# Multiplying rows by their reciprocal root mean square on GpSimd in place of VectorE

## The chip, the core and the metric

The kernel runs on one core of a Trainium2 chip, as one launch. The metric is the device time of that launch in microseconds (us). Engines are named as in the profile: PE is TensorE's matmul, PEld its weight load, DVE is VectorE, ACT is ScalarE, POOL is GpSimd, SP is the engine that issues the DMAs.

## What is computed

A batch of one with 256 tokens of width 1024, in float32, goes through two layers of a first block (four kinds of attention, then a mixture of 16 experts) and two layers of a second block. The second block is where the change lies. It has two layers of three sublayers each: a gated feed-forward network, a mixer (an mLSTM in the first layer, a Mamba-2 scan in the second) and another feed-forward network. Cut to what matters:

```
def rms_norm(x, g):
    y = x * rsqrt(mean(x * x, axis=-1) + EPS)
    return y * g

def sublayer(x, fn, g_pre, g_post, shift, scale, gate, weight):
    hmod = rms_norm(x, g_pre) * (1 + scale) + shift
    y = rms_norm(fn(hmod), g_post)
    return x + weight * gate * y
```

In the Mamba-2 mixer the scan's output, multiplied by silu(z), is normed in the same way within each of four groups of 512 columns before the last projection.

## The kernel before

The 256 tokens are two row tiles, t = 0 and t = 1, of 128 partitions each. A matmul needs the activations with the contracted dimension on the partitions, so the function `make_xT` brings rows into that form. It takes four blocks of 128 columns at a time (a group, 512 columns), transposes them on PE into one PSUM bank (line 204), and takes them from there into SBUF as two parts: a rounded part `xTh`, cast by ACT (line 397), and the rest `xTl`, a subtraction on DVE (line 398). Three matmuls, of the two parts with the two parts `hi` and `lo` of the weights, then make one product (line 200). The weights' parts are made in the same way: ACT casts `hi` (line 290) and DVE subtracts to get `lo` (line 293); both inputs of that subtraction lie in SBUF.

Where `make_xT` is given a factor `r`, one per row, it first multiplies the group by it into a tile named `rr` (line 381); PE then transposes `rr`. Two places give it a factor:

- `sub_pre`, at the entry of each of the six sublayers, for each t: two groups of 512 columns, so 24 multiplies. ACT sums the squares (line 1470), DVE adds the two sums (line 245), POOL raises the result to the power -1/2 (line 246), and that is `r`. After the transposes, DVE (first group, line 393) and ACT (second group, line 395) put scale and shift on, into `xTm`.
- `gate` in `mamba`, for four groups of 512 columns and each t: one multiply each, so eight. There DVE makes the mean (line 236) and POOL the power (line 238).

A sublayer's last matmuls run over t = 0 first, then t = 1, and `sub_pre` for t is called as soon as the rows of t are done. So the entry of t = 0 runs beside the matmuls of t = 1, and the entry of t = 1 beside the next sublayer's first matmuls on t = 0. The first of the six entries follows a layer norm (lines 918 to 932; its factor comes from POOL's line 238) that ends the first block.

The order of the instructions on each engine is put together by a planner, from the order of the program, priorities that the code sets in places, and its own estimates of what each instruction takes. Each engine then runs its own list in that order and waits on semaphores. All loads of weights are issued from SP's queue; POOL issues no DMA here.

Of the kernel before, what the change touches and what calls it, by code (L numbers as in the profile page):

```python
# [16 lines left out]
OP = mybir.AluOpType  # L17
# [3 lines left out]
P = 128  # L21
# [113 lines left out]
class K:  # L135
# [236 lines left out]
    def make_xT(self, rows, t, xT, kt=KT, r=None, k0=0, mod=None, bank=None, hold=None):  # L372

        nc = self.nc
        for g in range(0, kt, 4):
            m = min(4, kt - g)
            ps = (bank or self.ps_tr)()[:, :m * P].rearrange("p (j q) -> p j q", j=m)
            c = rows[:, g * P:(g + m) * P]
            if r is not None:
                c = self.take([m * P], "rr")  # L380
                nc.vector.tensor_scalar(c, rows[:, g * P:(g + m) * P], r, None, OP.mult)
            for j in range(m):
                self.tr(ps[:, j], c[:, j * P:(j + 1) * P])
            if r is not None:
                self.give(c)
            i, o = divmod(k0 + g, 4)
            h, l = (x[i][:, o:o + m, t * P:(t + 1) * P] for x in xT)
            if mod is not None:
                src = self.take([4, P], "xTm")
                for j in range(m):  # L390
                    a, b = mod[1][:, g + j:g + j + 1], mod[0][:, g + j:g + j + 1]
                    if g == 0:
                        nc.vector.tensor_scalar(src[:, j], ps[:, j], a, b, OP.mult, OP.add)  # L393
                    else:
                        nc.scalar.activation(src[:, j], ps[:, j], AF.Identity, bias=b, scale=a)  # L395
                ps = src[:, :m]
            first = nc.scalar.copy(h, ps)  # L397
            second = nc.vector.tensor_sub(l, ps, h.bitcast(F32))  # L398
            if mod is not None:
                self.entry = second  # L400
            if hold:
                self.holds = {"s": [[EARLY_S, None], [99, first]], "v": [[MID_V, second]]}
            if mod is not None:
                self.give(src)
# [1614 lines left out]
```

## Time and profile before

| | us |
|---|---|
| median of three runs | 2161.49 |
| lowest and highest of the three | 2154.83, 2166.03 |
| the profiled execution's own time | 2156.63 |
| its span, first to last instruction | 2154.9 |

| engine | busy us | share of the span | instructions |
|---|---|---|---|
| PE | 2009.5 | 93% | 10417 |
| PEld | 1463.1 | 68% | 10417 |
| DVE | 1226.0 | 57% | 2049 |
| ACT | 834.2 | 39% | 1359 |
| POOL | 63.4 | 3% | 108 |

The span is one execution's; 1.7 us of the execution's own time lie outside it. Busy shares are averages over stages that differ, and work on one engine overlaps that on the others, so the columns don't add up to the span. What one instruction is worth is read from the wait that ends last at its place.

### The profile page before, as it was taken

Reading aid. Unit: us, or ns where it says so; the run is one execution under the profiler, and the core shown is the slowest. Engines: PE = TensorE matmul, PEld = TensorE weight load, DVE = VectorE, ACT = ScalarE, POOL = GpSimd, SP = SyncE. Lnnn points to the kernel's source line nnn. Section 1 sums busy time; section 2 is a strip of 40 time slices with the busy share of each in tenths; the row PEclk is TensorE's granted clock in tenths of the full one; section 3 lists DMA queues with packets and bytes.
Section 4 is the critical chain, followed back from the end, with each engine's and each line's share of the span. In section 5 each row is a group of like instructions: output and inputs, shape, how many; then the busy total and the mean of one; then the engine's idle time right before and its main releaser. Section 6 shows DMA issues by size and latency. Waiting matters only on the chain.

```text
span 2154.9 us, 28260 instructions
## 1 busy us (share of the span) xinstructions
PE 2009.5 (93%) x10417; PEld 1463.1 (68%) x10417; DVE 1226.0 (57%) x2049; ACT 834.2 (39%) x1359; POOL 63.4 (3%) x108
## 2 busy tenths in 40 slices
PE   7998899989997999979998979999999898998998
PEld 6866543338776443257786867777778797876887
DVE  5876411137776311177657776677667578655544
ACT  5543100024443100054334554345444456745442
POOL 1000000010000000000000000000000000000000
PEclk9998899999998999989998989999999999999999
DMA  6854799986755999968847746874786343334662
GB/s 226 318 160 150 278 410 411 411 335 226 256 176 193 364 409 410 410 207 272 270 161 262 254 147 203 275 261 150 252 281 219 110 129 117 104 136 143 188 209 82
DMA packets 214232, 515.85 MB, mean 239 GB/s; under 512 B 23562, under 2 KB 36936, under 8 KB 214088
## 3 DMA queue, kind: packets, MB, share of 16 engines
q1 hardware_dynamic: 214088, 513.98, 68.4%
q8 instruction: 84, 1.38, 0.3%
q14 instruction: 60, 0.49, 0.1%
HBM read 512.87 MB, written 1.05 MB: 238 GB/s over the span
## 4 chain that ended last, share of the span: by engine, by line
PE 45%; DMA 4%; DVE 4%; ACT 2%; issue 1%; POOL 0%; SPq 0%; DVEq 0%; POOLq 0%; ACTq 0%
PE ps L200 39%; PE ps L122 4%; DMA w<-in_ffn_w_dram 2%; DVE lo L293 2%; PE ps L204 1%; DMA w<-in_mb_w_in_dram 1%; DMA adaw<-in_ada_w_dram 1%; ACT hi L290 1%; DMA w<-in_ml_w_in_dram 1%; DVE xTm L393 0%; DVE lo L297 0%; ACT xTm L395 0%; DVE xTl L398 0%; PE ps L1411 0%; DVE adac L1447 0%
## 5 line engine op out<-in xcount | busy, mean ns | idle before, releaser
L200 PE MATMUL ps<-hi,xTh 128*128 128x512 f32 (+3 forms) x1632 | 641.7, 397 | 38.4 <-ACT xTh L397 24.0
L200 PE MATMUL ps<-hi,xTl 128*128 128x512 f32 (+3 forms) x1632 | 636.3, 390 | 7.5 <-DVE xTl L398 7.2
L293 DVE TENSOR_TENSOR lo<-w,hi 128x1024 fp32r<-128x1024 f32 (+2 forms) x458 | 482.0, 1074 | 271.1 <-ACT hi L290 261.5
L290 ACT CAST hi<-w 128x1024 fp32r<-128x1024 f32 (+2 forms) x458 | 416.3, 931 | 511.4 <-DMA w<-in_ffn_w_dram 331.4
L200 PE MATMUL ps<-lo,xTh 128*128 128x512 f32 (+3 forms) x1632 | 611.1, 387 | 0.9 <-DVE lo L293 0.6
L200 PEld LDWEIGHTS ps<-hi,xTh 128*128 128x128 f32 x1632 | 315.6, 194 | 112.6 <-ACT xTh L397 29.8
L200 PEld LDWEIGHTS ps<-hi,xTl 128*128 128x128 f32 x1632 | 316.8, 194 | 76.9 <-DVE xTl L398 13.6
L200 PEld LDWEIGHTS ps<-lo,xTh 128*128 128x128 f32 x1632 | 313.2, 192 | 66.2 <-DVE lo L293 2.0
L200 PE MATMUL ps<-w,xe 128*32 128x512 f32 (+2 forms) x1088 | 222.8, 597 | 1.7 <-DMA w<-in_w_dram 1.5
L1447 DVE SCALAR_TENSOR_TENSOR adac<-adaw,cact,adac 128x512 f32<-128x512 f32 x252 | 187.4, 748 | 13.8 <-DMA adaw<-in_ada_w_dram 9.8
L200 PEld LDWEIGHTS ps<-w,xe 128*32 128x32 f32 (+2 forms) x1088 | 65.5, 124 | 131.0 <-issue 110.4
L200 PE MATMUL ps<-w,hT 128*32 128x512 f32 (+2 forms) x520 | 132.8, 599 | 0.0
L122 PE MATMUL ps<-xTh,hi 128*128 128x256 f32 x384 | 112.4, 294 | 7.3 <-DVE dr L559 3.5
L122 PE MATMUL ps<-xTh,lo 128*128 128x256 f32 x384 | 111.3, 290 | 0.4 <-DVE lo L293 0.4
L122 PE MATMUL ps<-xTl,hi 128*128 128x256 f32 x384 | 109.9, 288 | 0.0
L1206 DVE TENSOR_TENSOR h<-h,ps 128x512 f32<-128x512 f32 (+1 forms) x14 | 9.6, 687 | 144.9 <-PE ps L200 143.7
L1228 ACT ACTIVATE yh<-ps,gs 128x512 fp32r<-128x512 f32 (+1 forms) x28 | 18.9, 686 | 186.0 <-PE ps L200 185.5
L200 PEld LDWEIGHTS ps<-w,hT 128*32 128x32 f32 (+2 forms) x520 | 38.0, 123 | 72.4 <-issue 59.4
L122 PEld LDWEIGHTS ps<-xTh,hi 128*128 128x128 f32 x384 | 75.2, 197 | 8.9 <-issue 4.0
L397 ACT CAST xTh<-ps 128x512 fp32r<-128x512 f32 (+1 forms) x84 | 42.7, 523 | 92.8 <-PE ps L204 89.7
L1229 DVE SCALAR_TENSOR_TENSOR yl<-ps,gs,yh 128x512 fp32r<-128x512 f32 (+1 forms) x28 | 20.7, 749 | 101.5 <-ACT yh L1228 101.0
L122 PEld LDWEIGHTS ps<-xTh,lo 128*128 128x128 f32 x384 | 75.4, 196 | 0.8 <-DVE lo L293 0.5
(350 smaller groups left out, 2014.2 us busy)
## 6 DMA issues: line engine op xcount, KB each, us to landing
w<-in_w_dram SPq DMA_DIRECT2D x378, 512.0 KB, 10.1
w<-in_ffn_w_dram SPq DMA_DIRECT2D x264, 512.0 KB, 4.6
adaw<-in_ada_w_dram SPq DMA_DIRECT2D x144, 512.0 KB, 4.9
w<-in_w_in_dram SPq DMA_DIRECT2D x60, 512.0 KB, 6.2
w<-in_mb_w_in_dram SPq DMA_DIRECT2D x40, 512.0 KB, 4.2
w<-in_ml_w_in_dram SPq DMA_DIRECT2D x24, 512.0 KB, 5.7
w<-in_w_out_dram SPq DMA_DIRECT2D x16, 512.0 KB, 5.7
w<-in_mb_w_out_dram SPq DMA_DIRECT2D x16, 512.0 KB, 3.3
```

What stands on the lines that cost most here:

```text
L122: self.k.nc.tensor.matmul(out, lhsT, rhs, start=not self.started, stop=stop)
L200: self.nc.tensor.matmul(out, lhsT, rhs, start=start, stop=stop)
L204: self.nc.tensor.transpose(out, in_, self.ident[:n, :n])
L290: self.nc.scalar.copy(hi[:, k], w[:, k])
L293: self.nc.vector.tensor_sub(lo[:, k], w[:, k], hi[:, k].bitcast(F32))
L397: first = nc.scalar.copy(h, ps)
L1206: V.tensor_mul(h[:m], h[:m], hp[1][:m])
L1228: nc.scalar.mul(yh[:m], py[n][:m], g)
L1229: V.scalar_tensor_tensor(yl[:m], py[n][:m], g, yh[:m].bitcast(F32), OP.mult, OP.subtract)
L1447: nc.vector.scalar_tensor_tensor(prev, wt[:, k], cc, prev, OP.mult, OP.add)
```

## The change

The multiply by `r` at line 381 goes to GpSimd. Operands, shapes and result stay as they are; the power on GpSimd (lines 238 and 246) stays where it is, so the factor is now made and used on the same engine.

```diff
             c = rows[:, g * P:(g + m) * P]
             if r is not None:
                 c = self.take([m * P], "rr")
-                nc.vector.tensor_scalar(c, rows[:, g * P:(g + m) * P], r, None, OP.mult)
+                nc.gpsimd.tensor_scalar(c, rows[:, g * P:(g + m) * P], r, None, OP.mult)
             for j in range(m):
                 self.tr(ps[:, j], c[:, j * P:(j + 1) * P])
```

## Rows read from the trace of the kernel before

**Rows 1.** Busy time by stretch; the second begins ahead of the first multiply.

```profile
core 0: us, PE busy (x) PEld busy (x) DVE busy (x) ACT busy (x) POOL busy (x), PEclk, DMA share, GB/s
925.00:2154.90 1229.90, 1153.79 (x5848) 947.37 (x5846) 812.88 (x1207) 584.42 (x900) 23.70 (x40) 0.96 0.59 191
```

**Rows 2.** The page's chain that ended last, shares by engine.

```profile
PE 45%; DMA 4%; DVE 4%; ACT 2%; issue 1%; POOL 0%; SPq 0%; DVEq 0%; POOLq 0%; ACTq 0%
```

**Rows 3.** DVE by line and shape: count, busy us and mean ns, idle before.

```profile
L293 DVE TENSOR_TENSOR lo<-w,hi 128x512 fp32r<-128x512 f32 x120 | 76.8, 685 | 29.1 <-ACT hi L290 29.1
...
L381 DVE TENSOR_SCALAR rr<-x,sm 128x512 f32<-128x512 f32 x24 | 10.6, 482 | 4.8 <-POOL sm L246 4.8
...
L381 DVE TENSOR_SCALAR rr<-y,sm 128x512 f32<-128x512 f32 x8 | 3.8, 480 | 1.5 <-POOL sm L238 1.5
```

**Rows 4.** Everything on tile rr: who waited for it (us, times).

```profile
  PE ps L204: 16.4, 4
...
  PEld ps L204: 2.6, 1
```

**Rows 5.** POOL by line and shape, its memsets.

```profile
L548 POOL MEMSET fqT<- 64x512 f32 x4 | 2.1, 520 | 17.2 <-PE ps L200 17.0
...
L1604 POOL MEMSET ur<- 128x128 f32 x2 | 0.4, 206 | 11.9 <-DVE xTl L398 11.3 <-ACT sq L1470 0.6
```

**Rows 6.** POOL's power on one column: ns of one, least/median/most.

```profile
L246 POOL TENSOR_TENSOR sm<-sm,cf x24: 550/551/1466, 933.7 to 2149.6; 128x1 f32<-128x1 f32 x24
```

**Rows 7.** The same for the power on four columns.

```profile
L620 POOL TENSOR_TENSOR sm<-sm,cf x16: 1007/1008/1502, 90.0 to 685.6; 128x4 f32<-128x4 f32 x16
```

**Rows 8.** Timeline at 1294 us: start us, us, engine, line, count [idle before].

```profile
1294.70 1.28 DVE L293 TENSOR_TENSOR lo<-w,hi 128x512 fp32r<-128x512 f32 x2
...
1294.93 1.47 POOL L246 TENSOR_TENSOR sm<-sm,cf 128x1 f32<-128x1 f32 x1 [4.99 <-DVE sm L245]
```

**Rows 9.** Timeline of POOL at the first entry.

```profile
933.72 0.55 POOL L246 TENSOR_TENSOR sm<-sm,cf 128x1 f32<-128x1 f32 x1 [3.11 <-DVE sm L245]
934.24 0.64 POOL L238 TENSOR_TENSOR sm<-sm,cf 128x1 f32<-128x1 f32 x1
938.73 0.55 POOL L246 TENSOR_TENSOR sm<-sm,cf 128x1 f32<-128x1 f32 x1 [3.86 <-DVE sm L245]
```

**Rows 10.** The chain from 929 to 957 us: start us, us, what.

```profile
935.04 0.88 DVE rr L381 x2
935.92 1.32 DVE x L932 x2
...
939.72 0.48 DVE rr L381
...
950.42 3.38 DVE lo L293 x6
...
954.72 0.61 DVE xTl L398
```

**Rows 11.** The chain from 1154 to 1167 us.

```profile
1155.69 1.42 DVE adac L1447 x2
1157.11 0.79 DVE rr L381 x2
...
1163.21 0.61 DVE xTl L398
```

**Rows 12.** The chain from 1698 to 1711 us.

```profile
1703.70 0.56 POOL sm L246
...
1704.29 0.50 DVE rr L381
...
1704.92 1.96 PE ps L204 x8
```

**Rows 13.** Timeline of PE: transposes of rr, with PE's idle time ahead of them.

```profile
939.86 1.11 PE L204 MATMUL ps<-cf,rr 128*128 128x128 f32 x4 [2.25 <-DVE rr L381]
...
1157.65 1.06 PE L204 MATMUL ps<-cf,rr 128*128 128x128 f32 x8 [0.25 <-DVE rr L381]
...
1505.48 1.03 PE L204 MATMUL ps<-cf,rr 128*128 128x128 f32 x8
...
1704.92 1.94 PE L204 MATMUL ps<-cf,rr 128*128 128x128 f32 x8 [4.08 <-DVE rr L381]
```

**Rows 14.** Timeline of DVE at 1504 us.

```profile
1504.06 0.88 DVE L381 TENSOR_SCALAR rr<-x,sm 128x512 f32<-128x512 f32 x2 [0.73 <-POOL sm L246]
```

## Prediction, made before the changed kernel was run

> **What bounds the kernel now.** I read the page's chain of waits first. PE carries most of what it names, DMA and DVE 4% each, POOL nothing [rows 2]. So the kernel is bound by TensorE's own work, and an elementwise instruction counts only where PE stands still for it. Next I read busy time by stretch. Nothing that the change touches runs ahead of 925 us; behind it PE is busy for 1153.8 of 1229.9 us [rows 1], so all of PE's idle time there is 1229.9 - 1153.8 = 76.1 us, and DVE, the engine that is relieved, is busy for 812.9, or 66%. Then I asked for everything on the tile rr: PE waited for it four times, 16.4 us together, and its weight load once [rows 4]. The reader is to see there that 20 chains hang on that tile (twelve entries, eight gates of the Mamba mixer), and PE stands still for it at four of them. Last I took the chain around these four to see whether the multiply, or what stands ahead of it, makes the wait [rows 10 to 12].
>
> **What leaves DVE.** 24 multiplies of 10.6 us and eight of 3.8 us [rows 3]: 14.4 us of DVE time. In pairs they overlap, two in 0.88 us [rows 14]. DVE's own idle time in front of them, waiting for POOL's power, is 4.8 + 1.5 = 6.3 us more [rows 3].
>
> **What POOL takes on.** The trace of before has no multiply on POOL, so its cost is bounded by POOL's nearest rows. From below: a memset of 512 columns takes 0.52 us, one of 128 columns 0.206 [rows 5], so 0.314 / 384 = 0.82 ns a column. An instruction that also reads won't be shorter than that, and 0.52 us is the lower end. For the fixed part of one that reads: the power takes 0.55 us on one column and 1.01 on four [rows 6, 7], so 0.153 us a column and 0.55 - 0.15 = 0.40 us besides. The column price of the power can't be that of one multiply: it would make 0.40 + 512 x 0.153 = 78.7 us of each, where DVE's multiply, one pass, costs 0.48 [rows 3]; that end I exclude, since a power is worked out in many steps and a product in one. I take fixed part plus one pass, 0.40 + 512 x 0.00082 = 0.82 us, as the multiply is nearest to the memset: a stream over 512 columns. The upper end is reading and writing one after the other, 0.40 + 2 x 0.42 = 1.24 us. So POOL gains 32 x 0.82 = 26 us on 23.7 busy ones in this stretch [rows 1] and is still nearly empty. It issues no DMA, so no load stands behind the multiplies; what does stand there is the next power.
>
> **Where a slower multiply is hidden.** POOL can start when its own power ends, with no trip to DVE's queue. Sixteen of the 20 chains have room: PE comes to the transposes later, in its own order, with no idle time in front of them. The tightest is at 1504 us. There DVE starts at 1504.06 [rows 14] and PE transposes at 1505.48 without idle time [rows 13]. POOL would have the first group at 1504.06 + 0.82 = 1504.88, the second at 1505.70, and PE needs the second half-way through its 1.03 us, at about 1505.9. So 0.2 us are left there, and at 1.24 us a multiply (second group at 1506.54) some 0.6 would be lost. The other fifteen have at least 1.4 us.
>
> **The four places that count.**
>
> (a) and (b), the first entry, 933 to 957 us. The chain is on DVE nearly throughout: two multiplies in 0.88 us, the layer norm of t = 1 behind them, the last multiply of t = 1 (0.48), then the subtractions and xTl, and PE waits for that [rows 10]. DVE is freed of 2 x 0.88 = 1.76 us there. Against it: t = 0's power ends at 934.27, and the power for t = 1's layer norm stands next on POOL and ends at 934.88 [rows 9]. If the two multiplies get in front of it, it ends at about 934.3 + 2 x 0.82 + 0.55 = 936.5, and the layer norm (935.92 now) starts some 0.6 us later. And t = 1's own multiply comes 0.82 - 0.48 = 0.34 us later to PE, which stands idle for it already [rows 13]. The subtractions of the weights, which need neither, can fill part of that. I put it at 1.76 - 0.6 - 0.34 = 0.8 us won; with all filled 1.76 are won, and with 1.24 us a multiply, 0.84 us later on top, none.
>
> (c) the second entry's t = 1, 1155 to 1164 us. Here the multiplies stand behind DVE's accumulations for another stage (1.42 us) and cost 0.79 us of DVE's chain, which ends in xTl and releases PE [rows 11]. Off DVE, 0.79 is the most that can be won; POOL has the power at 1156.2 and could be done at 1156.2 + 0.82 = 1157.0, ahead of DVE's 1157.5. I take 0.6 us, since ACT's part of the entry also stands in front of PE; at the lower end nothing.
>
> (d) the fifth entry's t = 1, 1704 us. The power ends at 1704.26, DVE's first product is there 0.5 us later, and PE, idle for 4.08 us, starts at once [rows 12, 13]. Nothing else is on DVE. POOL's product takes 0.82: 0.34 us lost, 0.76 at the upper end, next to nothing at the lower.
>
> The sum: - 0.8 - 0.6 + 0.34 = - 1.1 us. With POOL at 0.52 it is - 1.76 - 0.79 = - 2.6; with POOL at 1.24, 0 + 0 + 0.76 + 0.6 (the place at 1504) = + 1.4. Against the profiled execution's own time that is 2156.6 - 1.1 = 2155.5. That execution lies 4.9 us below the median of the runs shown, 2161.5, so as a median I expect 2160.4, and write 2160.
>
> **Contention, a rule that speaks against the change.** Rows first: a power on POOL that takes 0.55 us took 1.47 where two subtractions with both inputs in SBUF ran on DVE; it ended 0.42 us behind the second [rows 6, 8]. So POOL is held while such an instruction runs on DVE. Whether DVE is held by POOL, no row of before shows: a power on one column reads too little. The Trainium skill (SBUF — State Buffer, Who interferes with whom) says that DVE and GpSimd share a port pair as an exclusive lock, that a DVE instruction with two SBUF inputs takes it against a GpSimd one that reads, and that whoever starts first blocks the other for its whole length. By it, each side would wait for the other; the rows agree with one half.
>
> **The rivals.**
>
> Contention in both directions, slower. Place: each of 32 multiplies holds the subtraction of DVE next to it for 0.82 us. At most that is 26.2 us of holds against 14.4 us saved, + 11.8 us, so 2173. Against it: only at (a) to (c), six multiplies, does DVE end the wait, so 6 x 0.82 = 4.9 us, which gives 2165 and no change that can be told. Over 0.5% slower, it needs (10.8 + 1.1) / 0.82, about 15 of the 32 holds on the path; DVE's 4% of the chain speaks against that. The 0.5% (10.8 us) is about what a measurement of this kernel can tell from no change: the three runs alone lie 11.2 us apart.
>
> DVE's relief counts everywhere, faster. If all 14.4 us and half of the 6.3 us of waits were on the path, 17.5 us would be won: 2144. For it: DVE is two thirds busy behind 925 us. Against it: at most of the entries DVE stands idle near the multiply, waiting for ACT's casts, which wait for DMA.
>
> The planner's other order. It knows POOL's multiply by another cost than DVE's, and everything behind 925 us may be put in another order, loads too. All it can move is PE's 76.1 us of idle time and the clock: the granted clock behind 925 us is 0.96 [rows 1], that is, most of it at 2.4 GHz and the rest at 1.2. A tenth of the idle time is 7.6 us, either way: 2153 to 2168. It passes 0.5% where a seventh of the idle time is added or taken away.
>
> No trace of it at all: everything is hidden, 2161.5. It can't be told from my forecast.
>
> **How the numbers follow.** My forecast or no trace at all, 0.64 together. Contention 0.14, of which 0.06 over the bound. Relief everywhere 0.06, of which 0.04 over it. The planner's order 0.16, of which 0.05 slower and 0.04 faster. So slower 0.11, faster 0.08, same 0.81. The time is the first case's, 2160. The range takes in the sum's ends (2158.9 to 2162.9), the spread of the runs, the planner's 7.6 us either way and most of contention's 11.8: 2149 to 2172. What is left out is the far end of relief and of contention.
>
> **What would show it.** Right: 32 multiplies on POOL of 0.5 to 1.2 us, none on DVE; PE idle in front of rr's transposes at the same four places, longer at 1704 by 0.3 us; the stretch ahead of 925 us unchanged; PE's busy time the same. Wrong: POOL multiplies of well over 1.24 us, or subtractions of 128x512 that take over 0.69 us beside them; new idle time of PE at the fifteen places with room; or a different order on PE and SP behind 925 us, with idle time elsewhere that no multiply explains.

## The result and the profile after

The changed kernel takes 2169.23 us (median of 20 runs, 2160.71 to 2174.54); the kernel before, beside it, 2155.05 (20 runs, 2147.75 to 2166.45). The ratio is 1.0053, 95% interval 1.004 to 1.0065: some 11 us slower by that ratio (the two medians lie 14.2 us apart), just past the 0.5% that the prediction set as its bound. The number lies inside the stated range, but on the wrong side of the kernel before; a change of - 0.07% had been forecast.

Busy time by stretch, in the columns of [rows 1]:

```profile
0.00:925.00 925.00, 856.64 (x4573) 515.97 (x4573) 413.26 (x843) 250.49 (x461) 39.63 (x68) 0.96 0.82 304
925.00:2162.40 1237.40, 1149.38 (x5846) 941.19 (x5844) 804.02 (x1175) 583.84 (x901) 82.15 (x72) 0.96 0.58 190
```

All of the time is lost behind 925 us: 1237.4 us against 1229.9 [rows 1] in the two profiled executions. PE's idle time there grew from 76.1 us to 1237.40 - 1149.38 = 88.0, while the granted clock stayed at 0.96. DVE has 32 instructions fewer and is busy for 8.9 us less; POOL's busy time went from 23.7 to 82.2.

Everything on the tile `rr`, least/median/most ns of one, then who waited for it (us, times):

```profile
L381 POOL TENSOR_SCALAR rr<-x,sm x24: 1558/1574/2646, 934.4 to 1966.7; 128x512 f32<-128x512 f32 x24
L381 POOL TENSOR_SCALAR rr<-y,sm x8: 1572/1574/2642, 1797.0 to 1914.5; 128x512 f32<-128x512 f32 x8
...
  PEld ps L204: 20.0, 7
  PE ps L204: 17.7, 5
```

One multiply takes 1.57 us on POOL, 3.3 times DVE's 0.48 [rows 3], and up to 2.65. PE waits for `rr` five times (17.7 us) where it was four (16.4), and its weight load, which runs ahead of the matmuls, so that its waits needn't be PE's, seven times (20.0) where it was once (2.6) [rows 4].

In the page's chain of waits POOL still has 0%, as in [rows 2]. Half a per cent of the time, spread over several places, is too little for such shares; the places have to be looked at one by one.

POOL's timeline at the first entry, which answers to [rows 9]:

```profile
933.16 0.55 POOL L246 TENSOR_TENSOR sm<-sm,cf 128x1 f32<-128x1 f32 x1 [3.11 <-DVE sm L245]
933.68 0.63 POOL L238 TENSOR_TENSOR sm<-sm,cf 128x1 f32<-128x1 f32 x1
934.39 3.74 POOL L381 TENSOR_SCALAR rr<-x,sm 128x512 f32<-128x512 f32 x2
938.10 0.56 POOL L246 TENSOR_TENSOR sm<-sm,cf 128x1 f32<-128x1 f32 x1
938.76 3.21 POOL L381 TENSOR_SCALAR rr<-x,sm 128x512 f32<-128x512 f32 x2
```

The layer norm's power (933.68) did keep its place ahead of the two multiplies. But the next power, t = 1's own factor at 938.10, follows the pair with no idle time: its input was ready when DVE's line 245 ended at 937.10 + 0.17 = 937.27 (first row below), so it stood 0.83 us behind the multiplies.

DVE's timeline there:

```profile
937.10 0.17 DVE L245 SCALAR_TENSOR_TENSOR sm<-sm 128x1 f32<-128x1 f32 x1 [0.85 <-ACT sq L1470]
...
951.61 5.44 DVE L293 TENSOR_TENSOR lo<-w,hi 128x512 fp32r<-128x512 f32 x8
956.96 0.70 DVE L398 TENSOR_TENSOR xTl<-xTm,xTh 128x512 fp32r<-128x512 f32 x1
957.56 1.30 DVE L1460 TENSOR_TENSOR dg<-cf,modc 128x512 f32<-128x512 f32 x2
958.76 0.70 DVE L398 TENSOR_TENSOR xTl<-xTm,xTh 128x512 fp32r<-128x512 f32 x1
```

The same place on DVE in the kernel before (the chain of [rows 10] ends in its second row):

```profile
945.61 9.11 DVE L293 TENSOR_TENSOR lo<-w,hi 128x512 fp32r<-128x512 f32 x15
954.64 1.29 DVE L398 TENSOR_TENSOR xTl<-xTm,xTh 128x512 fp32r<-128x512 f32 x2
955.84 1.29 DVE L1460 TENSOR_TENSOR dg<-cf,modc 128x512 f32<-128x512 f32 x2
```

Before, both halves of t = 1's `xTl` were made together, ahead of `dg` (line 1460, a tile for the rows of the gate); after, the second half stands behind `dg` and is done at 959.46, not at 955.93. Nothing in these rows is a multiply: the order of DVE's list has changed.

PE's timeline, its waits at the first entry, at 1507 us (1505 before), at 1709 us (1705 before) and at the last entry:

```profile
936.64 1.12 PE L204 MATMUL ps<-cf,rr 128*128 128x128 f32 x4 [11.35 <-POOL rr L381]
938.18 1.12 PE L204 MATMUL ps<-cf,rr 128*128 128x128 f32 x4 [0.42 <-POOL rr L381]
939.87 0.79 PE L200 MATMUL ps<-hi,xTh 128*128 128x512 f32 x1 [0.57 <-ACT xTh L397]
...
959.52 0.50 PE L200 MATMUL ps<-hi,xTl 128*128 128x512 f32 x1 [4.01 <-DVE xTl L398]
...
1507.45 0.66 PE L204 MATMUL ps<-cf,rr 128*128 128x128 f32 x4 [0.72 <-POOL rr L381]
...
1708.88 1.12 PE L204 MATMUL ps<-cf,rr 128*128 128x128 f32 x4 [4.80 <-POOL rr L381]
...
1957.88 1.22 PE L200 MATMUL ps<-hi,xTh 128*128 128x512 f32 x2 [7.97 <-ACT xTh L397]
1962.34 0.80 PE L200 MATMUL ps<-hi,xTl 128*128 128x512 f32 x1 [3.23 <-DVE xTl L398]
```

The waits of the kernel before at the first and the last entry that the rows ahead of the prediction don't hold:

```profile
935.67 1.94 PE L204 MATMUL ps<-cf,rr 128*128 128x128 f32 x8 [9.82 <-DVE rr L381]
...
955.38 0.50 PE L200 MATMUL ps<-hi,xTl 128*128 128x512 f32 x1 [1.26 <-DVE xTl L398]
...
1951.17 1.22 PE L200 MATMUL ps<-hi,xTh 128*128 128x512 f32 x2 [5.47 <-ACT xTh L397]
1952.98 0.79 PE L200 MATMUL ps<-hi,xTl 128*128 128x512 f32 x1 [0.58 <-DVE xTl L398]
...
1968.11 0.65 PE L204 MATMUL ps<-cf,g 128*128 128x128 f32 x4 [1.26 <-DVE xTm L393]
```

The wait for `xTl` at the first entry grew from 1.26 to 4.01 us, and those for `xTh` and `xTl` at the last entry from 6.05 to 11.20. None of these is a wait for `rr`. Other waits at the same two entries went away (2.25 us for `rr` of t = 1 [rows 13], 1.26 at 1968 us and 0.20 right behind it), so that the first entry's waits grew in all from 13.3 to 16.4 us and the last one's from 7.5 to 11.2: 6.7 us of the 11.9 that PE's idle time grew by.

A third place is the Mamba mixer, where PE waits for the tile `e` (line 1844, DVE). Who waited for `e` (us, times), in the changed kernel:

```profile
  PE ps L122: 9.6, 5
```

The same in the kernel before:

```profile
  PE ps L122: 2.9, 1
```

Other waits shrank there too: all of PE's waits in the mixer, from 1715 to 1920 us, came to 13.2 us before and to 16.1 after. At 1507 us and 1709 us the waits are for `rr` (0.72 where there was none, 4.80 where it was 4.08 [rows 13]).

So there are two suspects: the slow multiply itself, and another order that came with it.

### The profile page after: what moved, and what is told of

Same layout as the page of the kernel before. It is cut to its first block, busy times and chain, and to the rows that moved or that the text cites. A ratio compares the mean times of both kernels' runs of the same rounds, so it can differ in the third digit from the quotient of the medians.

```text
span 2162.4 us, 28272 instructions
## 1 busy us (share of the span) xinstructions
PE 2006.0 (93%) x10417; PEld 1457.2 (67%) x10417; DVE 1217.3 (56%) x2017; ACT 834.3 (39%) x1360; POOL 121.8 (6%) x140
## 5 line engine op out<-in xcount | busy, mean ns | idle before, releaser
L1447 DVE SCALAR_TENSOR_TENSOR adac<-adaw,cact,adac 128x512 f32<-128x512 f32 x252 | 187.9, 750 | 14.2 <-DMA adaw<-in_ada_w_dram 10.3
L122 PEld LDWEIGHTS ps<-xTl,hi 128*128 128x128 f32 x384 | 75.3, 197 | 0.3
```

What stands on the lines that cost most here:

```text
L122: self.k.nc.tensor.matmul(out, lhsT, rhs, start=not self.started, stop=stop)
L1447: nc.vector.scalar_tensor_tensor(prev, wt[:, k], cc, prev, OP.mult, OP.add)
```

## The experiments

In all of them line numbers are those of the kernel before. Where an order is "kept", the program is planned twice: once with the multiply at line 381 on one engine, from which each engine's order behind 925 us is read, and a second time with the multiply on another engine and everything else chained, by ordering alone, in the order read. The 32 multiplies themselves go where the planner puts them. That separates what the order costs from what the multiply costs.

### Order and engine crossed

Order of before, multiplies on GpSimd:

```diff
+PLAN, RUN, FREE = "vector", "gpsimd", []
...
+        if i.engine in last:
+            tc.add_manual_dep(i, last[i.engine], mybir.DependencyInfo(mybir.DependencyClass.NoSync, mybir.DependencyReason.DATA), reason="keep_order")
+        last[i.engine] = i.name
...
-                nc.vector.tensor_scalar(c, rows[:, g * P:(g + m) * P], r, None, OP.mult)
+                FREE.append(getattr(nc, MUL).tensor_scalar(c, rows[:, g * P:(g + m) * P], r, None, OP.mult).ins.name)
...
+    _, order = program(host, PLAN)
+    nc, _ = program(host, RUN, order)
```

> The multiplies run on GpSimd, and every other engine keeps, instruction by instruction, the order that it had in the kernel before; GpSimd's own order is that of the changed kernel. Theory 1 (the loss is the planner's other order behind 925 us): within 0.15% of the kernel before, 3 us or less. Theory 2 (the loss is the multiply itself, 1.57 us in place of 0.48, at the places where PE waits for it): as the changed kernel, some 10 us or 0.5% slower. Between them lies what the places where PE waits add up to, with 1.57 us in my own sum: 4 to 6 us, 0.2 to 0.3%.

Measured: 2168.8 us against 2156.51, ratio 1.0055 (1.0034 to 1.0076). The slow multiply, in the order of before, costs by itself as much as the whole change. PE's timeline of this kernel, its waits for `rr`:

```profile
940.34 1.12 PE L204 MATMUL ps<-cf,rr 128*128 128x128 f32 x4 [11.35 <-POOL rr L381]
941.88 1.12 PE L204 MATMUL ps<-cf,rr 128*128 128x128 f32 x4 [0.42 <-POOL rr L381]
945.31 1.11 PE L204 MATMUL ps<-cf,rr 128*128 128x128 f32 x4 [2.31 <-POOL rr L381]
947.77 1.12 PE L204 MATMUL ps<-cf,rr 128*128 128x128 f32 x4 [0.93 <-POOL rr L381]
...
1513.84 0.66 PE L204 MATMUL ps<-cf,rr 128*128 128x128 f32 x4 [0.89 <-POOL rr L381]
...
1716.69 1.11 PE L204 MATMUL ps<-cf,rr 128*128 128x128 f32 x4 [4.89 <-POOL rr L381]
1718.23 1.11 PE L204 MATMUL ps<-cf,rr 128*128 128x128 f32 x4 [0.43 <-POOL rr L381]
```

The first entry: 11.35 + 0.42 + 2.31 + 0.93 = 15.0 us of idle time against 9.82 (PE's wait for t = 0, in the timeline of before) + 2.25 [rows 13] = 12.1, so 2.9 lost. PE's wait for `xTl` behind them, 1.26 us before, is gone in this run, which leaves 1.7 lost at this entry. Between an entry's two groups PE now stands still a second time (0.42, 0.93), because POOL hands over the second product 1.5 us and more after the first.

Order of after, multiplies on VectorE:

```diff
-PLAN, RUN, FREE = "vector", "gpsimd", []
+PLAN, RUN, FREE = "gpsimd", "vector", []
```

> The reverse: the multiplies run on VectorE, and every other instruction keeps the order that it has in the changed kernel. Theory 1 (order): as slow as the changed kernel, 0.4 to 0.6% slower than before. Theory 2 (the multiply itself): within 0.15% of the kernel before.

Measured: 2166.91 us against 2156.51, ratio 1.005 (1.0033 to 1.0067). The other order, with the multiplies as fast as before, costs as much too. PE's timeline of this kernel shows the very waits of after at the first and the last entry, with no multiply on POOL:

```profile
960.85 0.79 PE L200 MATMUL ps<-hi,xTl 128*128 128x512 f32 x1 [4.39 <-DVE xTl L398]
...
1968.69 1.22 PE L200 MATMUL ps<-hi,xTh 128*128 128x512 f32 x2 [8.85 <-ACT xTh L397]
1973.14 0.80 PE L200 MATMUL ps<-hi,xTl 128*128 128x512 f32 x1 [3.23 <-DVE xTl L398]
```

So both suspects are guilty, and they don't add up: the changed kernel has both and is as slow as either. PE waits for `rr` for 24.2 us with the slow multiplies in the order of before, and for 17.7 in that of after: the order of after leaves the multiply more time. That this room is what the order costs fits, but no run shows it.

### Which multiplies, in the order of before

GpSimd for ten multiplies alone: both t of the first entry, and t = 1 of the second, fourth and fifth, the places that the prediction named (the four that count and the tightest one, at 1504 us).

```diff
-                FREE.append(getattr(nc, MUL).tensor_scalar(c, rows[:, g * P:(g + m) * P], r, None, OP.mult).ins.name)
+                FREE.append(getattr(nc, MUL(len(FREE))).tensor_scalar(c, rows[:, g * P:(g + m) * P], r, None, OP.mult).ins.name)
...
-PLAN, RUN, FREE = "vector", "gpsimd", []
+PLAN, RUN, FREE = lambda k: "vector", lambda k: "gpsimd" if k in (0, 1, 2, 3, 6, 7, 14, 15, 18, 19) else "vector", []
```

The number `k` counts the multiplies in the order of the program.

> Order of the kernel before on all engines but GpSimd. GpSimd does only the ten multiplies of the five places that my sum named: the first entry (both row tiles), t = 1 of the second, fourth and fifth entries; the other 22 stay on VectorE. If the loss with the order kept (0.55%, 12 us) comes from PE waiting for the longer multiply at these places, most of it is here: 0.25 to 0.5% slower. Rival (holds and displaced instructions at all 20 places): a third of it, below 0.2%.

Measured: 2165.54 us against 2158.21, ratio 1.0035 (1.0015 to 1.0055).

The other 22 on GpSimd, these ten on VectorE (the same edit with "vector" and "gpsimd" exchanged in the second list):

> The complement, in the same order: GpSimd does the 22 multiplies at the places where PE comes later anyway, VectorE the ten others. If those are hidden: within 0.15% of the kernel before. Rival: two thirds of the loss, 0.3% or more.

Measured: 2157.86 us against 2158.21, ratio 1.0004 (0.9988 to 1.002). Two thirds of the multiplies can move to an engine that takes three times as long, and no loss is seen (the interval ends at 0.2%, 4 us); nor is anything won by what DVE no longer does. This run also shows that keeping an order by such chains costs nothing that can be told from none. Not all of the 22 are hidden, though. PE waits for `rr` at t = 0 of the fourth entry, where POOL's pair of multiplies took 4.81 us:

```profile
1486.36 0.66 PE L204 MATMUL ps<-cf,rr 128*128 128x128 f32 x4 [1.57 <-POOL rr L381]
```

### Which part of the order

All the multiplies run on VectorE here. An order planned with the multiplies on ScalarE:

```diff
-                FREE.append(getattr(nc, MUL).tensor_scalar(c, rows[:, g * P:(g + m) * P], r, None, OP.mult).ins.name)
+                FREE.append((nc.scalar.mul(c, rows[:, g * P:(g + m) * P], r) if MUL == 'scalar' else nc.vector.tensor_scalar(c, rows[:, g * P:(g + m) * P], r, None, OP.mult)).ins.name)
```

> The multiplies run on VectorE, and every other instruction keeps the order that the planner makes when the multiplies are ScalarE's: a third order, planned for a multiply of another engine and length. If the changed kernel's order loses because it is planned around a long multiply on GpSimd, this one lies nearer to the kernel before: within 0.25%. If the kernel before simply has a good order and any other is worse: 0.3 to 0.6% slower, like the order of the changed kernel.

Measured: 2158.62 us against 2158.21, ratio 1.0005 (0.9988 to 1.0021). An order other than that of before isn't slower for being another.

An order planned with GpSimd at the first entry's four multiplies only:

```diff
-PLAN, RUN, FREE = "gpsimd", "vector", []
+PLAN, RUN, FREE = lambda k: "gpsimd" if k < 4 else "vector", lambda k: "vector", []
```

> All multiplies on VectorE; the order of everything else is what the planner makes when it plans the first entry's four multiplies for GpSimd and the other 28 for VectorE. In the changed kernel's order with VectorE's multiplies, PE waited 4.39 us for xTl of the first entry's t = 1, against 1.26 before. If the order's loss sits there: PE waits some 4 us at that place again, 3 us or 0.15% slower than before. Rival (the order's loss is spread over all entries): at most 0.05%.

Measured: 2162.51 us against 2156.46, ratio 1.0028 (1.0008 to 1.0048). PE's timeline has the long wait for `xTl` at the first entry and, at the last, 4.86 + 1.03 us, near the 6.05 of before:

```profile
960.29 0.79 PE L200 MATMUL ps<-hi,xTl 128*128 128x512 f32 x1 [5.03 <-DVE xTl L398]
...
1955.50 1.22 PE L200 MATMUL ps<-hi,xTh 128*128 128x512 f32 x2 [4.86 <-ACT xTh L397]
1957.75 0.79 PE L200 MATMUL ps<-hi,xTl 128*128 128x512 f32 x1 [1.03 <-DVE xTl L398]
```

An order planned with GpSimd everywhere but at the first and the last entry:

```diff
-PLAN, RUN, FREE = "gpsimd", "vector", []
+PLAN, RUN, FREE = lambda k: "vector" if k < 4 or k >= 28 else "gpsimd", lambda k: "vector", []
```

> The complement: all multiplies on VectorE, order planned with GpSimd's multiplies everywhere but in the first and the last entry. In the changed kernel's order the last entry's idle time of PE was 12.1 us with VectorE's multiplies, against 7.3 before; with the first entry's 3 that makes 8 of the order's 11 us. If that is the loss: within 0.2% of the kernel before. Rival (spread): 0.3 to 0.5% slower.

Measured: 2155.52 us against 2156.46, ratio 1.0 (0.9985 to 1.0015). From the second entry to the fifth this order is for the most part that of after, and no cost is seen there. In the Mamba mixer it isn't: DVE's list there is in part that of before. Who waited for `e` (us, times), in the order of after with VectorE's multiplies:

```profile
  PE ps L122: 8.5, 4
```

The same in this kernel:

```profile
  PE ps L122: 2.6, 1
```

The order's cost therefore lies at the first entry, at the last entry and in the Mamba mixer, where PE's new waits are; the runs don't tell which of the last two. What either costs alone was not run; for both together it follows only from 1.005, 1.0028 and 1.0, whose intervals are wide beside the differences.

### Contention, and the multiply's own price

The order of before with every multiply on VectorE, and 32 more multiplies of the same rows on GpSimd into a spare tile that nobody reads; this adds work and takes none away (the order is read from a program without the extra ones):

```diff
-                nc.vector.tensor_scalar(c, rows[:, g * P:(g + m) * P], r, None, OP.mult)
+                nc.vector.tensor_scalar(c, rows[:, g * P:(g + m) * P], r, None, OP.mult); FREE.extend(nc.gpsimd.tensor_scalar(self.spare, rows[:, g * P:(g + m) * P], r, None, OP.mult).ins.name for _ in range(MUL))
```

> The kernel before in its own order, with its multiplies on VectorE; GpSimd does each of the 32 multiplies a second time, into a spare tile that nothing reads. Theory 3 (contention: a multiply on GpSimd holds VectorE's instructions with two inputs in SBUF, and that is the loss): 0.3% slower or more, subtractions of 128x512 beside a multiply at 0.95 to 1.0 us in place of 0.685. Theories 1 and 2: within 0.15% of the kernel before, the same stretched subtractions, but few of them where PE waits.

Measured: 2158.52 us against 2156.51, ratio 1.001 (0.9992 to 1.0029). The tiles `spare` and `rr`, least/median/most ns of one:

```profile
L381 POOL TENSOR_SCALAR spare<-x,sm x24: 1562/1861/2593, 934.3 to 1962.7; 128x512 f32<-128x512 f32 x24
```

```profile
L381 DVE TENSOR_SCALAR rr<-x,sm x24: 474/764/918, 934.4 to 1961.1; 128x512 f32<-128x512 f32 x24
```

Each engine holds the other: the median of DVE's multiply of `x` went from 0.481 to 0.764 us, POOL's from 1.574 to 1.861. All of it together costs no time that can be told from none. As nobody reads `spare`, this is the cost of what is held on DVE; what PE loses when POOL is held, the run doesn't show.

The same with the extra multiplies cut to 128 columns (first groups and the mixer's) and 256 (second groups):

```diff
-nc.gpsimd.tensor_scalar(self.spare, rows[:, g * P:(g + m) * P], r, None, OP.mult)
+nc.gpsimd.tensor_scalar(self.spare[:, :(g + 4) * 32], rows[:, :(g + 4) * 32], r, None, OP.mult)
```

> One look at the price of a multiply: as the run with the extra multiplies, but the extra one covers 128 columns where it stands for a first group and 256 where it stands for a second. By my rows of before (0.40 us fixed, the rest by columns), 1.57 us for 512 columns means 2.3 ns a column: 0.69 us for 128 columns and 0.99 for 256. If the fixed part is the larger than I took it: both nearer to 1.57.

One execution, 2158.09 us. The least for 128 columns is 0.612 us:

```profile
L381 POOL TENSOR_SCALAR spare<-y,sm x8: 612/978/1297, 1792.1 to 1911.4; 128x128 f32<-128x128 f32 x8
```

With 1.558 us as the least for 512 columns, a column costs (1.558 - 0.612) / 384 = 2.46 ns, and 0.612 - 128 x 0.00246 = 0.30 us are fixed.

### Without the multiply

The factor is put into the identity that the transposes use: rows times a diagonal matrix, on PE. The multiplies of rows are left out and 20 small ones make the diagonals.

```diff
-                c = self.take([m * P], "rr")
-                nc.vector.tensor_scalar(c, rows[:, g * P:(g + m) * P], r, None, OP.mult)
+                dr = self.take([P], "dr") if g == 0 else dr
+                nc.vector.tensor_scalar(dr, self.ident, r, None, OP.mult) if g == 0 else None
...
-                self.tr(ps[:, j], c[:, j * P:(j + 1) * P])
+                self.tr(ps[:, j], c[:, j * P:(j + 1) * P]) if r is None else self.mm(ps[:, j], c[:, j * P:(j + 1) * P], dr)
```

> No multiply of rows at all: VectorE scales the 128x128 identity by the factor once for each entry and row tile, and the transposes become matmuls by that diagonal. 20 scalings of 128 columns at about 0.2 us take the place of 32 multiplies of 0.48. If DVE's multiply costs anything on the path (1.4 us and 0.8 us of the chain at the first and second entries, 0.5 at the fifth), this wins up to 3 us, 0.1%; the planner makes a new order, which by theory 1 can move it by 0.5% either way; by theory 2 it stays within 0.15%.

Measured: 2163.8 us against 2156.51, ratio 1.0025 (1.0006 to 1.0044). The tile `dr`:

```profile
L200 PE MATMUL ps<-dr,x x192: 270/275/582, 937.4 to 1973.4; 128*128 128x128 f32 x192
L200 PE MATMUL ps<-dr,y x64: 270/275/377, 1794.0 to 1921.2; 128*128 128x128 f32 x64
```

256 matmuls stand where the trace of after has 128 transposes: each product with the diagonal is two matmuls in the trace. Behind 925 us PE is busy for 1169.4 us where it was 1153.8 [rows 1], while its idle time there, 70.2 us of 1239.6, is 5.9 us less than before. This takes work from an engine with room and gives it to the one that bounds the kernel. The planner's order is a new one here as well, so the run doesn't price the products by themselves.

No kernel here is faster than the one before. The order planned for ScalarE's multiplies, that of the middle entries, the 22 multiplies moved and the extra ones can't be told from it.

## Why the prediction was wrong

**The step that failed first: the price of one multiply on POOL.** The prediction took 0.82 us and closed the range at 1.24 ("reading and writing one after the other"). It is 1.57 us alone, and up to 2.65 beside DVE. The fixed part was near (0.40 taken, 0.30 measured); the price of a column was not: 0.82 ns, from memsets [rows 5], against 2.46. A memset only writes, and no row supported the choice "nearest to the memset"; the other neighbour, the power with 153 ns a column [rows 6, 7], was excluded with a sound reason, but the whole distance between the two was then given to the lower one. "POOL multiplies well over 1.24 us" was named as the first sign of a wrong prediction, and it is what the trace shows.

**What follows from it at the places.** (a) and (b), put at 0.8 us won and at worst nothing, are 1.7 us of PE's idle time lost in the order of before (2.9 at `rr`, less the 1.26 at `xTl` that went away). The 0.6 us taken off for multiplies that get in front of the layer norm's power was the wrong wait: that power kept its place, and in the changed kernel it was t = 1's own that stood behind them, for 0.83 us. The upper end of this term was too good by itself, too: at 1.24 us t = 1's own multiply also comes 0.42 us later, which the sum left out, so that 0.4 us would have been lost there and not none. (c), put at 0.6 won, is nothing: there PE waits 1.10 and 0.88 us for `rr` and 2.10 and 0.58 for the two parts, 4.66 together, where before it was 0.25 for `rr` [rows 13] and 2.94 and 1.44, 4.63. (d), put at 0.34 lost, is 4.89 + 0.43 - 4.08 = 1.2 lost; its direction was right. The tightest of the hidden places, put at 0.6 lost for a dear multiply, shows a wait of 0.89. That makes 3.8 us by PE's waits for `rr` and what follows them, inside the interval of the ten multiplies moved alone (0.15 to 0.55% of 2158 us, 3.2 to 11.9 us) but only half of its middle, 7.6. The right price in the prediction's own sum would thus have turned its sign, but by itself would have stayed under the 0.5%.

**The step that failed second: the planner's order.** It was left out of the sum and stood as a rival with a chance of 0.16, "either way", and with 7.6 us in the range. Its mechanism was told rightly: a different order behind 925 us and idle time of PE that no multiply explains. But it was no coin to be tossed. It cost 0.50% (0.33 to 0.67) with the multiplies on VectorE. At two places DVE's list shows what changed: at the first entry `xTl` of t = 1 stands behind one more subtraction (21 where it was 20) and its second half behind `dg`; at the last entry `xTl` stands behind two more subtractions and the addition to the rows (line 1488), which it stood ahead of before. The Mamba mixer, with its longer waits for `e`, is the third. That the planner allowed for a long multiply and so gave its followers later places is likely, but its estimates are on no record here. The prediction asked what the planner's price could do to the time, and not what the same price would do to the lists around the four places that it had itself found to be tight.

**What was right.** Elementwise work counts only where PE stands still for it: 22 of the 32 multiplies moved at no cost that is seen, and in the changed kernel PE itself stands still for `rr` only at the first entry, at 1507 us and at 1709 us, all of them named. ("Sixteen have room" doesn't hold in the order of before: at t = 0 of the fourth entry, one of them, PE waited 1.57 us with the 22 moved and 1.03 with all 32.) DVE's relief is worth nothing: it has 8.9 us less to do behind 925 us, and the 22 gain nothing. The stretch ahead of 925 us is unchanged.

**Contention.** The prediction weighed it at 0.14 and at no more than 4.9 us where DVE ends the wait. On DVE's side it is small: the 120 subtractions of 128x512 take 78.1 us in the changed kernel where it was 76.8 [rows 3], and the extra multiplies cost 0.10% of the time, - 0.08 to 0.29, so that up to 6 us aren't excluded.

```profile
L293 DVE TENSOR_TENSOR lo<-w,hi 128x512 fp32r<-128x512 f32 x120 | 78.1, 698 | 30.3 <-ACT hi L290 28.4 <-PE ps L200 1.6
```

The other side, which the prediction saw but didn't price, is part of what a multiply costs. POOL's two pairs at the first entry, in the order of before with all multiplies on GpSimd:

```profile
938.09 3.73 POOL L381 TENSOR_SCALAR rr<-x,sm 128x512 f32<-128x512 f32 x2
...
943.68 4.04 POOL L381 TENSOR_SCALAR rr<-x,sm 128x512 f32<-128x512 f32 x2
```

The pair at 1715 us of that run took 3.11, so 0.6 and 0.9 us of the longer waits for `rr` at this entry can be POOL held by DVE, and not the multiply's own price. In the changed kernel the pair ahead of the wait at 1507 us took 4.13.

The Trainium skill (SBUF — State Buffer, Who interferes with whom) calls the port pair that DVE and GpSimd share an exclusive lock, and says of DVE's two-port modes that whoever issues first has it for the whole instruction and the other is blocked fully. In the changed kernel both sides are held, but on DVE's side by less than that. The timelines of DVE and POOL at 1486 us:

```profile
1486.12 4.61 DVE L293 TENSOR_TENSOR lo<-w,hi 128x512 fp32r<-128x512 f32 x6 [0.72 <-ACT hi L290]
```

```profile
1486.13 4.34 POOL L381 TENSOR_SCALAR rr<-x,sm 128x512 f32<-128x512 f32 x2
```

Five such subtractions in a row take 3.09 us in the kernel before and thirteen 7.91 in this one, so one more costs 0.60 and six take 3.7; beside two multiplies of 1.57 they took 4.61, 0.9 more and not the 3.1 of both multiplies. POOL's two took 4.34 where the pair at 938.76 us took 3.21, 1.1 more.

**What stays open.** One execution differs from another by a few us in its waits for loads, so places were read from single traces and sizes from the intervals. The order of before with all 32 on GpSimd costs 0.55% (0.34 to 0.76), the ten named ones 0.35 and the others 0.04; the intervals allow that these add up, and also that some 3 us come from elsewhere. PE's waits for `rr` at the named places come to 3.8 us; where the rest of those 0.55%, some 8 us by its middle, arises is not located. How the order's cost divides between the first entry, the Mamba mixer and the last entry is not settled.

## What to carry to other kernels

Where no row shows an operation on its new engine, the bound must reach at least to several times the price on the old one, and the tightest place worked out with that; a write-only neighbour is no price for an instruction that reads. Where a planner orders the lists, a dearer operation changes the order around it as well, and that alone can cost as much as the operation: run the old order with the new engine, and the new order with the old engine, before you name a cause. Moving the instructions that PE hardly waits for cost nothing that could be seen here, but it brought nothing either, because the engine relieved was not the bound.

## What the runs showed of the hardware

GpSimd's multiply of 128x512 float32 by one factor a row takes 1.57 us, 0.61 for 128 columns: 2.46 ns a column, where VectorE's takes 0.48 us for 512. GpSimd and VectorE hold each other in both directions, and in part: beside the extra multiplies VectorE's own went from 0.48 to between 0.47 and 0.92 us, and GpSimd's from 1.56 up to 2.59. With one after the other, a pair of GpSimd's multiplies took from 3.11 us to 4.81 in these traces.
